# One over the RMS by columns, embedding products pinned between output projection and FFN, attention pools laid out anew: a float32 encoder kernel on one core

## The chip, the core and the metric

The kernel runs on one core of a Trainium2 chip. The metric is the device time of one launch in microseconds (us). Five engines work side by side, each on its own queue of instructions in a fixed order: PE (TensorE, matrix products), DVE (VectorE), ACT (ScalarE), POOL (GpSimd) and SP (SyncE), which here only issues DMA transfers. They wait for one another through semaphores, so an instruction that waits also holds all that stands behind it in its queue.

## What is computed

Two layers of an encoder over 1024 positions with 1024 channels, all in float32. Layer 0 has differential attention, layer 1 windowed attention with four query heads to one key head. Each layer runs:

```python
hn = rms_norm(h, attn_norm[i])
if i % N_MIXERS == 0:
    mix = diff_attention(hn, diff_w_qkv[j], diff_w_o[j], diff_lambda[j], diff_subln[j], cos, sin, i)
else:
    mix = windowed_gqa(hn, swa_w_qkv[j], swa_w_o[j], swa_sinks[j], cos, sin)
h = h + mix
h = h + conv_ffn(rms_norm(h, ffn_norm[i]), ffn_w_up[i], ffn_conv_w[i], ffn_conv_b[i], ffn_w_down[i])
gate = jax.nn.sigmoid(rms_norm(h, ple_norm[i]) @ ple_w_gate[i])
h = h + (p[i] @ ple_w_proj[i]) * gate
```

`rms_norm` divides each position by the root of its mean square. A last `rms_norm` follows layer 1. `p[i] @ ple_w_proj[i]` (1024 x 256 by 256 x 1024) is called the embedding product below; it needs nothing of `h`.

## The kernel before

Activations lie transposed: 8 tiles of 128 channels by 1024 positions, worked on in two halves (hf 0 and 1) of 512 positions. Every float32 operand is split into a high part (a cast on ACT) and a low part (a subtraction on DVE or POOL), and each product is three matmuls of 128 x 128 by 128 x 512 (`mm3`, L237 to L239). Weights come through a ring of buffers: raw `wr`, high `wh`, low `wl`, two of each. The up-projection computes its two-by-two blocks with seven products in place of eight (m1 to m7, L1107 to L1109), which need sums of the weights (`seven_weights`, L1071 to L1081, tiles sf, wd, w) and of the activations (`seven_begin`, `seven_rest`: tiles q, qb, ta, tb, qa, qu). Up-projection weights come in 22 groups, j.

The stages of a layer, in order: `qkv0` or `qkv1` (queries, keys, values, stored to memory), the attention (`diff_attn`, `swa`), `out_proj` with the residual add, the embedding product `p_proj`, `ffn_up`, `ffn_down`, and the gate (`ple0`, or `ple1_final` at the end). `projected` holds out_proj, p_proj and ffn_up together.

The order of the instructions on each engine is set by a scheduler ahead of time, from a program order and modelled durations; it is fixed then, and every queue runs in it. `out_proj` computes the first four row tiles for both halves, then the last four for half 0, then for half 1 (`half_order`). Each adds its old residual (read back from memory, `old`), squares the result on ACT (L472) and sums the squares on DVE into nacc (L473). When a half is complete, `norm_half` makes one over the RMS for it: a matmul of ones by nacc (L499) gives the sum over channels in every row of a 128 x 512 tile, DVE scales it (L500), ACT takes Ln (L502) and Exp (L503), each after a table load, and DVE makes a Newton step (L477 to L479). Where the same numbers are wanted as columns, four transposes (L511) and a copy (L512) turn them (`rstd_cols`). In `p_proj`, p is transposed on PE (L1282), split, and multiplied; the sums are copied by ACT (L1303) into two tiles pp of 128 x 1024 and stored. DVE then normalises the residual (L1010) for the up-projection.

Memory for the tiles of the attentions comes from pools with one place each (`attn_pools`); the order of the names decides which earlier tiles lie beneath a place, and so what its first load must wait for.

## Time and profile before

| | us |
|---|---|
| median of 3 runs | 2752.45 |
| lowest, highest | 2751.73, 2758.04 |
| the profiled execution, its own time | 2753.88 |
| its span, first to last instruction | 2752.1 |
| PE busy in it | 2633.3 |
| DVE, ACT, POOL busy | 1947.6, 1226.2, 1076.2 |
| mean granted clock of PE | 0.985 of 2.4 GHz |

Time between a row's start and the next start on the same engine tells what an instruction costs there; matmuls are pipelined, so the duration shown for one (about 0.39 us for 512 columns) is longer than the distance of two starts. A name such as `ps<-gh,wh` is the output tile and its inputs. What stands in brackets behind a row is the engine's idle time ahead of it and the instruction that ended the idle time.

### The profile page before, as it was taken

What the parts mean: (1) busy time and instruction counts of PE and PEld (TensorE: products, weight loads), DVE (VectorE), ACT (ScalarE), POOL (GpSimd) and SP (SyncE); (2) the same over time, 40 slices, a digit from 0 to 9 for tenths busy, and PEclk for the clock granted to TensorE, in tenths of its full rate; (3) what the DMA queues carried; (4) which work ended last, traced back from release to release, by engine and by line L of the source; (5) the groups of instructions that cost most, each with busy time, mean ns of one, the idle gap of its engine ahead of it and who ended that gap; (6) DMA issues with size and microseconds to landing.
All of it is one profiled execution on the core that took longest, in us unless ns stands there. A gap on an engine that the chain in (4) does not pass through costs nothing. (4 is left out here: it accounts for less than half of the span.)

```text
span 2752.1 us, 33264 instructions
## 1 busy us (share of the span) xinstructions
PE 2633.3 (96%) x12606; PEld 2184.3 (79%) x12606; DVE 1947.6 (71%) x2276; ACT 1226.2 (45%) x2133; POOL 1076.2 (39%) x609
## 2 busy tenths in 40 slices
PE   8999899999889999999999998999899999999998
PEld 6888788888678888878888787888678888788877
DVE  7640478784598888866677755874888888856664
ACT  5322577773444444441145525873444444421152
POOL 2642477774023443425312443441133434334201
PEclk9999999999999999999999999999899999999999
DMA  6445323303322323234314446103323223344112
GB/s 227 163 152 173 109 79 108 96 12 111 114 88 78 92 70 92 90 140 142 104 46 138 145 151 225 47 28 119 130 69 92 78 84 92 117 143 138 62 65 97
DMA packets 201828, 296.23 MB, mean 108 GB/s; under 512 B 9268, under 2 KB 138437, under 8 KB 197957
## 3 DMA queue, kind: packets, MB, share of 16 engines
q1 hardware_dynamic: 201045, 293.72, 32.5%
q8 instruction: 99, 1.62, 0.2%
q14 instruction: 60, 0.49, 0.1%
q10 hardware_dynamic: 624, 0.39, 0.0%
HBM read 207.83 MB, written 86.25 MB: 107 GB/s over the span
## 5 line engine op out<-in xcount | busy, mean ns | idle before, releaser
L148 POOL TENSOR_TENSOR wl<-wr,wh 128x1024 fp32r<-128x1024 f32 (+1 forms) x113 | 295.3, 2630 | 651.2 <-ACT wh L142 594.5
L1071 POOL TENSOR_TENSOR sf<-wr 128x1024 f32<-128x1024 f32 x42 | 136.2, 3244 | 549.9 <-DVE w L1081 549.9
L1237 DVE TENSOR_TENSOR res<-res,ps 128x512 f32<-128x512 f32 x320 | 217.0, 684 | 146.2 <-PE ps L239 143.5
L237 PE MATMUL ps<-gh,wh 128*128 128x512 f32 x704 | 272.9, 391 | 5.2 <-DVE ug L1178 4.0
L239 PE MATMUL ps<-gh,wl 128*128 128x512 f32 x704 | 274.4, 390 | 0.0
L238 PE MATMUL ps<-gl,wh 128*128 128x512 f32 x704 | 274.4, 390 | 0.0
L237 PE MATMUL ps<-hn,wh 128*128 128x512 f32 x544 | 215.1, 396 | 4.9 <-ACT wh L142 4.9
L238 PE MATMUL ps<-hn,wh 128*128 128x512 f32 x544 | 213.6, 393 | 0.0
L239 PE MATMUL ps<-hn,wl 128*128 128x512 f32 x544 | 212.9, 393 | 0.1
L142 ACT CAST wh<-wr 128x1024 fp32r<-128x1024 f32 (+1 forms) x140 | 144.7, 1091 | 124.2 <-PE ps L238 68.7
L748 ACT ACTIVATE e<-S,sm 128x1024 f32<-128x1024 f32 x128 | 142.4, 1114 | 92.8 <-DVE sm L744 91.0
L142 ACT CAST gh<-gr 128x1024 fp32r<-128x1024 f32 x44 | 46.1, 1051 | 295.4 <-PE ps L239 214.2
L1080 ACT CAST w<-sf 128x1024 fp32r<-128x1024 f32 x88 | 92.6, 1052 | 177.7 <-PE ps L1109 104.6
L744 DVE TENSOR_REDUCE sm<-S 128x1 f32<-128x1024 f32 x128 | 152.5, 1216 | 24.7 <-PE S L743 23.6
L237 PEld LDWEIGHTS ps<-gh,wh 128*128 128x128 f32 x704 | 132.2, 188 | 35.0 <-issue 4.8
L239 PEld LDWEIGHTS ps<-gh,wl 128*128 128x128 f32 x704 | 132.4, 188 | 27.5
L760 POOL TENSOR_TENSOR e<-e,e 128x1024 f32<-128x1024 f32 x64 | 152.1, 2377 | 5.3
L238 PEld LDWEIGHTS ps<-gl,wh 128*128 128x128 f32 x704 | 132.5, 188 | 27.1
L1107 PE MATMUL ps<-qb,w 128*128 128x512 f32 x352 | 138.7, 394 | 13.2 <-ACT pp L1303 9.9
L1109 PE MATMUL ps<-qa,w 128*128 128x512 f32 x352 | 138.0, 392 | 2.9 <-DVE w L1081 2.9
L1108 PE MATMUL ps<-qb,w 128*128 128x512 f32 x352 | 137.8, 392 | 0.0
L1108 PE MATMUL ps<-qa,w 128*128 128x512 f32 x352 | 137.7, 391 | 0.1
(260 smaller groups left out, 7283.0 us busy)
## 6 DMA issues: line engine op xcount, KB each, us to landing
wr<-ffn_w_up SPq DMA_DIRECT2D x88, 512.0 KB, 5.2
gs<-c SPq DMA_DIRECT2D x44, 512.0 KB, 2.9
wr<-ffn_w_down SPq DMA_DIRECT2D x22, 1024.0 KB, 5.1
gr<-gs SPq DMA_DIRECT2D x44, 512.0 KB, 3.7
qs<-rhl SPq DMA_DIRECT2D x32, 512.0 KB, 3.1
wr<-diff_w_qkv SPq DMA_DIRECT2D x12, 1024.0 KB, 5.9
ks<-rhl SPq DMA_DIRECT2D x20, 512.0 KB, 3.1
spill<-res SPq DMA_DIRECT2D x16, 512.0 KB, 2.6
```

What stands on the lines that cost most here:

```text
L142: self.nc.scalar.copy(out, in_)
L148: eng.tensor_tensor(out, in_, f32(hi), op=ALU.subtract)
L237: self.nc.tensor.matmul(out, ah, bh, start=first, stop=False)
L238: self.nc.tensor.matmul(out, ah, bl, start=False, stop=False)
L239: self.nc.tensor.matmul(out, al, bh, start=False, stop=last)
L744: v.tensor_reduce(sm[:, a : a + 1], ps[:], axis=AX.X, op=ALU.max, negate=True)
L748: nc.scalar.activation(e[:], ps[:], AF.Exp, bias=sm[:, a : a + 1], accum_out=sm[:, 2 + a : 3 + a])
L760: nc.gpsimd.tensor_tensor(ea[:], ea[:], eb[:], op=ALU.add)
L1107: mm(ps, ah, bh, start=first and i == 0, stop=False, skip_group_check=True)
L1108: mm(ps, ah, bl, start=False, stop=False, skip_group_check=True)
L1109: mm(ps, al, bh, start=False, stop=last and i == n - 1, skip_group_check=True)
L1237: v.tensor_tensor(self.res[dt][:, sl], self.res[dt][:, sl], acc[:], op=ALU.add)
```

## The change

1. **One over the RMS by columns.** `norm_half` becomes `norm_steps` and `spread_cols`. Four matmuls with one output column each (a 128 x 128 block of nacc as weights, a column of ones as data) give the sums as columns, 128 x 4. DVE scales them and POOL raises them to the power -1/2. DVE multiplies them into a diagonal matrix, a matmul of ones by it spreads them over all rows, and DVE copies the result. Ln, Exp, the Newton step and the transposes of `rstd_cols` are gone; `x_rstd` at the start uses the same spreading.
2. **The embedding product.** The transposes and splits of p go between the two halves of out_proj, its weights are fetched during half 1, and the 16 units of six matmuls run after out_proj, in memory pools of their own (three tiles pp of 128 x 512, 16 stores). The first matmul of each unit is kept in program order, and so are the norm's instructions of half 1: two units, the column matmuls, the remaining steps of `seven_begin`, two units, the spreading matmul, then twelve units. The first group of up-projection weights is fetched before the units, and its sums are on POOL (before, group 0 had them on DVE). In ffn_up's group 0, m1 and m2 are computed whole first. `old` has four buffers of its own.
3. **Attention pools.** New orders of places for both.
4. **Smaller pieces.** `ffn_down` takes its banks in another order and raises the priority of the loads of its first group; `qkv1`'s first weights are fetched and cast in `ple0`, between two blocks of half 1.

On PE, out_proj's end in layer 0 (ps is a sum's bank, wh and wl weights or parts of p, nacc the sum of squares). Before:

```order
L239 MATMUL ps_6288<-wh_6249,wl_6282 128x512
L239 MATMUL ps_6306<-wh_6249,wl_6282 128x512
L239 MATMUL ps_6314<-wh_6249,wl_6282 128x512
L499 MATMUL ps_6238<-nacc_5760,ones 128x512
L239 MATMUL ps_6324<-wh_6249,wl_6282 128x512
L239 MATMUL ps_6332<-wh_6249,wl_6282 128x512
L239 MATMUL ps_6342<-wh_6249,wl_6282 128x512
L239 MATMUL ps_6350<-wh_6249,wl_6282 128x512
L237 MATMUL ps_6360<-wh_6249,wh_6281 128x512
```

After (qb holds the parts of p now):

```order
L239 MATMUL ps_6366<-qb_5531,wh_6190 128x512
L242 MATMUL ps_6366<-qb_5531,wh_6190 128x512
L243 MATMUL ps_6366<-qb_5531,wl_6191 128x512
L239 MATMUL ps_6366<-qb_5532,wh_6190 128x512
L242 MATMUL ps_6366<-qb_5532,wh_6190 128x512
L243 MATMUL ps_6366<-qb_5532,wl_6191 128x512
L509 MATMUL ps_6375<-ones,nacc_5764 128x1 x4
L239 MATMUL ps_6390<-qb_5531,wh_6190 128x512
L242 MATMUL ps_6390<-qb_5531,wh_6190 128x512
```

The sum for the norm stood alone among products of p taken piece by piece; now its four column matmuls (the row with x4) stand between two whole units.

On SP, between qkv0 and the differential attention (vs is the store of v, stk a stack of queries or keys, wr a weight). Before:

```order
L646 DMA vs<-vf_1995 128x512
L646 DMA vs<-vf_2023 128x512
L646 DMA vs<-vf_2051 128x512
L646 DMA vs<-vf_2079 128x512
L620 DMA stk_2188<-qs_224 128x2048
L620 DMA stk_2189<-ks_228 128x2048
L169 DMA wr_5931<-diff_w_o 128x8x256
```

After:

```order
L642 DMA stk_2183<-ks_228 128x2048
L171 DMA wr_5797<-diff_w_o 128x8x256
L668 DMA vs<-vf_1905 128x512
L668 DMA vs<-vf_1933 128x512
L668 DMA vs<-vf_1961 128x512
L642 DMA stk_2182<-qs_224 128x2048
L644 DMA stk_2184<-ks_228 64x2048
L645 DMA stk_2184<-ks_228 64x2048
L743 DMA v_2189<-vs 128x8x128
L743 DMA v_2540<-vs 128x8x128
```

The loads of the stacks stood behind the stores of v; now they stand among them.

On DVE, the norm of half 1 in layer 0. Before:

```order
L148 TENSOR_TENSOR wl_6250<-ps_6251,wh_6249 128x512
L148 TENSOR_TENSOR wl_6250<-ps_6258,wh_6249 128x512
L473 TENSOR_TENSOR nacc_5760<-nacc_5760,old_6169 128x512
L148 TENSOR_TENSOR wl_6250<-ps_6265,wh_6249 128x512
L473 TENSOR_TENSOR nacc_5760<-nacc_5760,old_6200 128x512
L148 TENSOR_TENSOR wl_6250<-ps_6272,wh_6249 128x512
L473 TENSOR_TENSOR nacc_5760<-nacc_5760,old_6231 128x512
L500 TENSOR_SCALAR nv_6237<-ps_6238 128x512
L477 TENSOR_TENSOR nv_6237<-rstd_6241 128x512
L478 SCALAR_TENSOR_TENSOR nv_6237<-nv_6237 128x512
L479 SCALAR_TENSOR_TENSOR rstd_6241<-nv_6237,rstd_6241 128x512
```

After:

```order
L1121 TENSOR_TENSOR w_1069_6319<-wr_6312,w_1069_6319 128x1024
L480 TENSOR_TENSOR nacc_5764<-nacc_5764,old_6144 128x512
L993 TENSOR_TENSOR res_5730<-ps_6150,old_6175 128x512
L480 TENSOR_TENSOR nacc_5764<-nacc_5764,old_6175 128x512
L480 TENSOR_TENSOR nacc_5764<-nacc_5764,old_6221 128x512
L480 TENSOR_TENSOR nacc_5764<-nacc_5764,old_6259 128x512
L1121 TENSOR_TENSOR wd_6328<-wr_6312,wd_6328 128x512
L1121 TENSOR_TENSOR wd_6742<-wr_6726,wd_6742 128x512
L518 TENSOR_SCALAR rcol_6080<-ps_6375 128x4
L532 TENSOR_TENSOR diag_6409<-identr,rcol_6080 128x512
L542 COPY rstd_6413<-ps_6411 128x512
```

The splits of p (wl) between the sums are gone, and the splits of up-projection weights (w, wd) stand there; the rows from L500 to L479 gave way to three.

The diff, cut to its core:

```diff
+P_BANKS = ["b0", "b1", "b4", "b5", "b6", "b7"]
+DOWN_BANKS = ["b0", "b1", "b2", "b4", "b6", "b7", "b3", "b5"]
...
+    def kept(self, ins):
+
+        return self.tc.keep_in_program_order(ins)
...
+    def norm_steps(self, st, hf, psum, order, pin):
...
+        for i in range(4):
+            pin(
+                nc.tensor.matmul(
+                    ps[:, i : i + 1], acc[:, i * P : (i + 1) * P], self.ones[:, 0:1],
+                    start=True, stop=True,
+                )
+            )
...
+            nc.vector.tensor_scalar(
+                rc, ps[:, :4], 1.0 / D, EPS, op0=ALU.mult, op1=ALU.add
+            )
...
+        nc.gpsimd.tensor_tensor(rc, rc, self.mhalf[:, 0:1].to_broadcast([P, 4]), op=ALU.pow)
+        yield
...
+    def spread_cols(self, rc, hf, tp, psum, order, pin):
...
+            nc.vector.tensor_tensor(
+                dg[:].rearrange("p (i q) -> p i q", i=4),
+                self.ident.unsqueeze(1).to_broadcast([P, 4, P]),
+                rc.unsqueeze(2).to_broadcast([P, 4, P]),
+                op=ALU.mult,
+            )
...
+        pin(nc.tensor.matmul(ps[:], self.ones[:], dg[:], start=True, stop=True))
         y = self.rstd_tile(hf)
-        nc.scalar.activation(a, v, AF.Ln)
-        nc.scalar.activation(y[:], a, AF.Exp, scale=-0.5)
-        self.rsqrt_newton(y[:], v, a)
...
+        pin(nc.vector.tensor_copy(y[:], ps[:]))
...
-        for i in range(4):
-            self.nc.tensor.transpose(ps[:, i, :], rstd[:, i * P : (i + 1) * P], self.ident)
-        self.nc.vector.tensor_copy(rc[:, hf * 4 : hf * 4 + 4], ps[:, :, 0])
...
-            t = tp.tile([P, 2, HS], F32, tag="t", name=self.nm("old"))
+            old = tp.tile([P, HS], F32, tag="o", name=self.nm("old"))
...
+        def finish(psum, order, others):
+            steps = self.norm_steps(st, 1, psum, order, self.kept)
+            self.step(others)
+            self.step(others)
+            next(steps)
+            while begin:
+                self.step(begin)
+            self.step(others)
+            self.step(others)
+            for _ in steps:
+                pass
+            return st["rstd"]
...
-        eng = nc.vector if hurry else nc.gpsimd
+        eng = nc.gpsimd
...
-            w = self.seven_weights(raw, fp, j < 1)
+            w = first if j == 0 else self.up_weights(layer, j, fp)
...
+                for m in order[:2]:
+                    prod(pm[m], m)
                 for k in kps:
-                    for m in order:
+                    for m in order[2:]:
...
-                acc = self.bank(psum)
+                acc = self.bank(psum, DOWN_BANKS)
...
+                if g == 0:
+                    with self.tc.high_priority(400):
+                        load(j)
...
-                self.mm3(ps[:], terms)
-                nc.scalar.copy(t[:, sl], ps[:])
-                if hf == 1:
-                    nc.sync.dma_start(out[rs, :], t[:])
+                self.mm3(ps[:], terms, True)
+                nc.scalar.copy(t[:], ps[:])
+                nc.sync.dma_start(out[r * P : (r + 1) * P, sl], t[:])
...
+        def late():
+            self.hurry = True
+            self.wk1 = self.wrope(self.wraw(self.io["swa_w_qkv"][0], D))
+            self.hurry = False
...
+                first = self.up_weights(layer, 0, fp)
...
+                    rstd = finish(psum, END_BANKS, pieces)
+                    while pieces:
+                        self.step(pieces)
...
-            ap = self.attn_pools(c, "a0", ["q0", "k0", "l0", "q1", "k1", "l1"])
+            ap = self.attn_pools(c, "a0", ["k0", "q0", "l0", "v", "a", "k1", "q1", "l1", "e"])
...
-            ap = self.attn_pools(c, "a1", ["k0", "q0", "k1", "q1"])
+            ap = self.attn_pools(c, "a1", ["e", "a", "k1", "q1", "v", "k0", "q0"])
```

Before, `attn_pools` put `"v", "a", "e"` ahead of the names that it is given.

## Rows read from the trace of the kernel before

**Rows 1.** page, part 1: busy time, share of the span, instructions of each engine.

```profile
PE 2633.3 (96%) x12606; PEld 2184.3 (79%) x12606; DVE 1947.6 (71%) x2276; ACT 1226.2 (45%) x2133; POOL 1076.2 (39%) x609
```

**Rows 2.** waits of PE: line, what it waited for: us in all, times, longest.

```profile
PE S L742 <- DMA stk<-ks: 7.4, 1, 7.4
PE S L881 <- issue: 6.4, 1, 6.4
...
PE S L881 <- ACT e L894: 8.5, 5, 5.3
...
PE ps L237 <- ACT wh L142: 5.2, 3, 4.2
...
PE ps L511 <- DVE rstd L479: 4.3, 1, 4.3
PE ps L237 <- DVE ug L1178: 4.0, 2, 2.1
...
PE ps L237 <- DVE res L977: 12.2, 4, 5.5
PE ps L1107 <- ACT pp L1303: 9.9, 2, 5.0
```

**Rows 3.** stretches: length; busy us (instructions) by engine, PE first; PEclk, DMA share, GB/s.

```profile
1521.00:1532.00 11.00, 6.81 (x21) 4.95 (x20) 10.73 (x13) 9.44 (x9) 3.55 (x2) 0.72 0.38 141
1655.00:1700.00 45.00, 31.53 (x194) 28.99 (x194) 21.88 (x35) 21.43 (x61) 11.65 (x19) 0.85 0.66 245
1920.00:1980.00 60.00, 46.06 (x176) 35.18 (x175) 48.22 (x60) 31.86 (x49) 12.48 (x5) 0.86 0.41 136
2000.00:2020.00 20.00, 20.00 (x89) 16.45 (x88) 18.67 (x20) 9.87 (x10) 4.82 (x3) 1.00 0.26 79
2644.00:2656.00 12.00, 7.16 (x28) 4.77 (x27) 7.28 (x12) 4.92 (x8) 0.44 (x1) 0.86 0.00 0
```

**Rows 4.** timeline of DVE, layer 1, before FFN: start, us, instruction [idle, releaser].

```profile
1921.95 0.68 DVE L977 TENSOR_TENSOR res<-ps,old 128x512 f32<-128x512 f32 x1
...
1926.76 2.78 DVE L148 TENSOR_TENSOR q<-res,q 128x512 fp32r<-128x512 f32 x1
...
1936.41 0.67 DVE L473 TENSOR_TENSOR nacc<-nacc,old 128x512 f32<-128x512 f32 x1
...
1944.79 0.69 DVE L500 TENSOR_SCALAR nv<-ps 128x512 f32<-128x512 f32 x1 [7.71 <-PE ps L499]
...
1951.63 5.39 DVE L1010 SCALAR_TENSOR_TENSOR res<-res,par,rstd 128x512 f32<-128x512 f32 x8
```

**Rows 5.** timeline of ACT, same stretch.

```profile
1947.49 1.28 ACT L503 ACT_TABLE_LOAD   x1
1948.78 0.63 ACT L503 ACTIVATE rstd<-nv 128x512 f32<-128x512 f32 x1
```

**Rows 6.** timeline of PE, same stretch.

```profile
1925.74 0.49 PE L1282 MATMUL ps<-identr,wr 128*128 128x128 f32 x3
```

**Rows 7.** timeline of POOL, same stretch.

```profile
1926.63 5.11 POOL L148 TENSOR_TENSOR wl<-wr,wh 128x1024 fp32r<-128x1024 f32 x2 [40.39 <-ACT wh L142]
```

**Rows 8.** groups by line on POOL: busy, mean ns; idle before.

```profile
L1071 POOL TENSOR_TENSOR sf<-wr 128x1024 f32<-128x1024 f32 x42 | 136.2, 3244 | 549.9 <-DVE w L1081 549.9
...
L687 POOL TENSOR_TENSOR ss<-ss,mhalf 128x4 f32<-128x4 f32 x16 | 16.3, 1019 | 3.1 <-DVE ss L684 1.8
```

**Rows 9.** one line on PE: duration ns min/median/max, starts.

```profile
L499 PE MATMUL ps<-nacc,ones x20: 590/592/595, 703.9 to 2664.9; 128*128 128x512 f32 x20
```

**Rows 10.** timeline of SP, before both attentions.

```profile
295.33 0.32 SPq L620 DMA_DIRECT2D stk<-ks  x1
...
1655.51 0.80 SPq L620 DMA_DIRECT2D q<-qs  x2
```

**Rows 11.** timeline of ACT, first exponential of the windowed attention.

```profile
1676.88 0.48 ACT L894 ACTIVATE e<-S,sm 128x257 f32<-128x257 f32 x1 [10.01 <-DMA vs<-vhl]
```

**Rows 12.** page, part 6: DMA issues, KB each, median us to landing.

```profile
wr<-ffn_w_up SPq DMA_DIRECT2D x88, 512.0 KB, 5.2
```

More of the change, by code (lines that the diff above doesn't have):

```diff
@@ L236, in mm3 @@
             last = i == n - 1
-            self.nc.tensor.matmul(out, ah, bh, start=first, stop=False)
+            ins = self.nc.tensor.matmul(out, ah, bh, start=first, stop=False)
+            if keep and first:
+                self.kept(ins)
             self.nc.tensor.matmul(out, ah, bl, start=False, stop=False)
@@ L466, in norm_tile @@
         if st["acc"][hf] is None:
-            acc = st["tp"].tile([P, HS], F32, tag="n", name=self.nm("nacc"))
+            pool = st["keep"] if hf == 1 and st["keep"] else st["tp"]
+            acc = pool.tile([P, HS], F32, tag="n", name=self.nm("nacc"))
             st["acc"][hf] = acc
@@ L493, in norm_half @@
     def norm_half(self, st, hf, psum, order):
+        for _ in self.norm_steps(st, hf, psum, order, lambda ins: ins):
+            pass
+    def norm_steps(self, st, hf, psum, order, pin):
         nc = self.nc
-        t = st["tp"].tile([P, 2, HS], F32, tag="t", name=self.nm("nv"))
-        v, a = t[:, 0], t[:, 1]
         ps = self.bank(psum, order)
-        nc.tensor.matmul(ps[:], self.ones[:], st["acc"][hf][:], start=True, stop=True)
-        nc.vector.tensor_scalar(v, ps[:], 1.0 / D, EPS, op0=ALU.mult, op1=ALU.add)
@@ L501, in norm_half @@
[L501 to L512 removed]
+        acc = st["acc"][hf]
@@ L944, in swa, with out_proj @@
             self.step(jobs)
-    def out_proj(self, w, hp, tp, psum, which, layer):
+    def out_proj(self, w, hp, tp, keep, psum, which, layer):
         nc = self.nc
@@ L1003, in half_order @@
                     unit(b, c, hf)
+                if hf == 1 and b == 2 and late is not None:
+                    late()
             done(hf)
+            if hf == 0 and middle is not None:
+                middle()
     def normed(self, layer, kt, hf, rstd):
@@ L1263, in ffn_down, with p_parts @@
                     self.norm_half(st, hf, psum, END_BANKS)
[L1264 to L1269 removed]
+        return st["hn"], st["rstd"], st["cols"]
+    def p_parts(self, layer, psum):
         nc = self.nc
```

217 lines of the change are left out of this document (111 added, 106 removed).

## The prediction

> **What bounds the kernel now.** I read the busy shares first: PE is busy 96% of the span and the next engine, DVE, 71% [rows 1]. So only two things can shorten the program: fewer PE columns, or less time in which PE stands or runs slowly. The change hardly touches the columns, so the next view is what PE waited for [rows 2]. The waits that matter are few, long and each at a border between two stages: the differential attention's first tile (7.4 us), the two waits before the windowed attention (6.4 and 5.3), the first products of qkv1 (4.2), the last norm (4.3), the two ffn_up to ffn_down borders (4.0 together), and above all, in both layers, the border from out_proj over the embedding products to ffn_up (12.2 and 9.9 in all). The third view, stretches, shows that a wait costs more than its length, since the granted clock falls behind it: in the undisturbed stretch it is 1.00 and 89 matmuls take 20.00 us, 0.225 us each, at full clock (2.4 GHz); in the stretches with a wait the mean is 0.72 to 0.86, that is, part of each ran at the lower level, 1.2 GHz [rows 3].
>
> From these I take as lost, in a stretch, its length less 0.225 us for each of its matmuls. 1920 to 1980: 60 - 176 x 0.225 = 20.4, and about 22 since 16 of the 176 are 128-wide transposes of half that time; the list of waits has its two long waits twice, once in each layer, so layer 0 counts the same. 1521 to 1532: 11 - 21 x 0.225 = 6.3. 2644 to 2656: 5.7. The windowed attention's matmuls are of several widths, so there I go by idle time: 1655 to 1700 has 45 - 31.5 = 13.5 us without PE work, and clock 0.85 [rows 3].
>
> **The change part by part.** The sum is made against the profiled execution's own 2753.88 us (span 2752.1); the median of the runs is 2752.45, so 1.4 is taken off at the end.
>
> *(a) Attention pools, layer 0.* The first loads stk are issued one after the other, the second at 295.33, behind the last use of the memory under them, and PE waits 7.4 us [rows 2, 10]. In the new order the two loads stand in the middle of the v products, ahead of the last stores of v, so they land under PE work. What is late next is ACT, which casts output weights until about then. Gain 7.5, from 5 to 9 (with less slow clock behind it).
>
> *(d) Attention pools, layer 1.* Two loads q are issued together at 1655.51, and PE waits 6.4 us [rows 2, 10]; then the first exponential is held to 1676.88 by the store of v, because its tile e lies over v's source, and PE waits 5.3 more [rows 2, 11]. After the change only k0 and q0 are in front, q1 comes later, and e lies elsewhere. Together 11.7 us of waiting and perhaps 3 of slow clock. I don't credit all: k0 and q0 still follow the last projections over SP, and the first exponential now needs a table load, since no Exp ran in the norm before. That load is 1.28 us [rows 5]. Gain 8.5, from 3 to 10.
>
> In that row the load ends at 1948.77 and the activation starts at 1948.78 [rows 5], so nothing follows it. The Trainium skill, "ScalarE: Activation LUTs", section "What ACT_TABLE_LOAD costs", adds a drain of 1380 ns to the 1283 ns of the load, 2.66 us for each switch. By that the first exponential would be 1.4 us later and the result 2707 instead of 2706; the trace does not show the drain, so the row decides.
>
> *(c) ple0 to qkv1.* PE waits 4.2 us for the cast of the first qkv1 weights, because ACT first runs the table loads and activations of the norms and of the gate [rows 2]. Afterwards there are no Ln and Exp, and the weights are fetched and cast between two blocks of ple0's second half, 24 matmuls ahead (5.4 us). The stretch loses 6.3 [rows 3]. Gain 7 with the half-clock part that lies outside the window, from 3 to 7.5.
>
> *(f) ffn_down to ple1_final.* PE waits 4.3 us for rstd, whose columns it must transpose; the chain is sum, Ln, Exp, Newton [rows 2]. By columns the transposes are gone. What is late next is the cast of the gate weights, which I put at 1.5 us (three waits on such casts come to 5.2 [rows 2]). The stretch loses about 6 and the clock stays low a little longer. Gain 5, from 2 to 6.5.
>
> *(b) ffn_up to ffn_down.* Two waits of about 2 us on a bank whose reader, DVE's ug, is late [rows 2]. The new order of banks takes others first, and the loads of the first group are raised. What is late next is DVE's uv just ahead, a wait that stays. Gain 3 for both layers, from 0 to 4.
>
> *(e) out_proj, embedding products, ffn_up.* This is the largest term. Before, p is transposed, split on DVE and multiplied while the norm of half 1 runs on DVE and ACT. PE waits 5.5 for DVE [rows 2], whose queue is full until the last nacc sum at 1936.41 [rows 4]; then ones x acc, scale at 1944.79, Ln, Exp, Newton, and the normalisation starts only at 1951.63 [rows 4, 5]. The eight stores of p's products and their two tiles give the second wait, 5.0 [rows 2].
> Afterwards, on layer 1's clock: before, the transposes of p end near 1926.5 [rows 6]; they now come earlier and shift out_proj by as much, so it ends near there, 1926.9. Two units of six matmuls take 2.7, to 1929.6. The next instruction on PE is the four pinned one-column matmuls, and nothing may pass them. They need nacc. From 1921.95 [rows 4] DVE has 19 operations of 0.67 or, started one behind the other, 0.60 us, and one of double width: 12.7 us, to 1934.6. To this I add 2.1: an operation of 0.67 took 2.78 beside GpSimd's wl [rows 4, 7], and the first sum of the up-weights, 3.24 us on GpSimd [rows 8], now falls into this queue. So nacc is ready at 1936.7 and PE waits 7.1. Slow clock behind it 2.4 (as behind the 5.5 now), the small matmuls 0.9. Then scale, pow (1.02, the same shape [rows 8]), diagonal, one ones x diag matmul (two records of 0.59 [rows 9], as before) and a copy: rstd at about 1943 instead of 1951.6, with two units of p beside it. Then twelve units (16.3 us) run beside the normalisation (5.4 [rows 4], perhaps 2 more beside GpSimd's second and third sum), then m1 and m2 (5.4). The weights of the other products come when p's weights have freed their buffer: 5.2 us of loading [rows 12], a cast and a split, about 1.8 later than PE. Lost afterwards 7.1 + 2.4 + 0.9 + 1.8 = 12.2, and 12.5 with rounding up for ones x diag out of line. Gain 22 - 12.5 = 9.5 in each layer, 19 together; bounds 0 (the new waits are as long as the old) and 18 a layer (nacc is ready when PE gets there).
>
> *Costs.* Eight further norm halves get four one-column matmuls of two records each. No row shows such a record; it is between nothing and the 0.59 of the 512-wide one [rows 9]. I take 0.1, nearer to nothing because the width is 1 against 512: 0.8 a half, 6.4 in all, part of it inside waits, against 16 transposes removed (1.8). Cost 3, from -1 to 8 (0.59 each would be 38, which I hold for excluded, since the record would not shrink with its width at all). GpSimd's pow, ten times 1.02, lies beside PE work except in (e). The old loads issued earlier, and the 16 instead of 8 stores of p's products, lie on SP beside PE work: nothing, and some us in the prologue if that cover is gone.
>
> **Sum.** 7.5 + 8.5 + 7 + 5 + 3 + 19 - 3 = 47. 2753.9 - 47 = 2706.9; against the median 2705.5, so 2706.
>
> **Rivals.**
> R1, as summed: 2706.
> R2, the FFN border returns nothing. For it: PE's order is pinned, so each us by which DVE's queue or a weight is late is a us of PE, and PE waits there longer (7.1 against 5.5) by my own account. Against: rstd comes 8 us earlier. 2706 + 19 = 2725.
> R3, the border closes. For it: DVE may clear its queue earlier, as p's four splits (four of 0.6) are gone from it. 2 x 18 = 36 instead of 19: 2689.
> R4, the change doesn't do what it says at the attentions: the loads are early in the queue but wait for other memory under the new places, or for v. Then (a) and (d) are lost: 2706 + 16 = 2722.
> R5, slower: the first up-projection weights. Their load stands on SP behind out_proj's stores, its cast on ACT ahead of two squares, its split on DVE ahead of all nacc sums but one, and these ahead of PE's pinned matmuls. If the load is late, ACT, DVE, and PE stand in turn. Counted is landing near 1927.5, 5.2 us after its buffer is free [rows 12]. Each us later is one us of PE in each layer; the 47 are used up when it lands 24 us later, and it is slower by over 0.3% (8.3 us, about what a measurement of this kernel can tell) from 28 us. Only a buffer that is freed by the products of p themselves would do that. About 2765.
>
> **How the numbers follow.** Chances: R1 0.52, R2 0.22, R3 0.12, R4 0.08, R5 0.06. Predicted is R1, 2706. The low end is R3 with the better bounds of (a), (c) and (d), 2689 - 5 = 2684. The high end is R2 with the lower bounds of (b), (d), (f), about half of them coming at once: 2725 + 10 = 2735. Beyond lie R5 and parts of R2 to R4. Within 0.3% would need R2 and R4 together, and half of (c) and (f) gone, 0.05; faster by over 0.3% 0.89, slower 0.06.
>
> **What would show it.** In the profile after: no wait of PE for stk above 2 us, and none of 5 for e (a, d); no wait for the cast in qkv1 (c); no transposes of rstd (f); in each layer one wait of about 7 at the one-column matmuls, for nacc, and one under 2.5 at ffn_up's third product (e). It is wrong if the pinned matmuls wait over 12 us, if DVE's operations beside GpSimd's sums take 2.8 in a row, if the differential attention's steps, which I hold unchanged, take longer, or if the first exponential of the windowed attention starts no sooner behind the last v product.

## The result, and the profile after

| | before | after |
|---|---|---|
| median of five runs each, us | 2751.73 | 2730.89 |
| ratio, with its 95% interval | | 0.9924 (0.9907 to 0.9940) |
| span of the profiled execution, us | 2752.1 | 2728.9 |
| mean granted clock of PE | 0.985 | 0.989 |

The kernel became faster by 21 us (23 by the spans). 46 were forecast, so the sign and the range held and the size did not: less than half of it came. One disturbed run of the kernel after, 3293.94 us, is left out of the ratio.

Read as before the change, the page's first part of the kernel after comes first (busy time, share, instructions):

```profile
PE 2637.1 (97%) x12670; PEld 2189.5 (80%) x12670; DVE 1929.6 (71%) x2250; ACT 1185.6 (43%) x2090; POOL 1102.4 (40%) x625
```

ACT lost 41 us of work, DVE 18, and PE has 64 more matmul records than in [rows 1]. The bound is the same, so again it is the waits of PE that count. These are the ones that answer to [rows 2] (line, what it waited for: us in all, times, longest):

```profile
PE ps L509 <- DVE nacc L480: 9.5, 3, 4.3
PE ps L239 <- DVE qb L150: 7.0, 2, 3.6
PE ps L1147 <- ACT pp L1357: 5.8, 2, 3.6
...
PE ps L239 <- DVE rcol L518: 3.0, 1, 3.0
PE S L897 <- ACT e L910: 2.8, 5, 0.7
...
PE ps L242 <- DVE gl L150: 2.2, 3, 1.0
...
PE ps L239 <- ACT wh L144: 1.2, 2, 0.7
```

Gone are the 7.4 for stk, the 6.4 and the 5.3 ahead of the windowed attention, the 4.2 for qkv1's cast, the 4.3 for rstd at the end and the 4.0 for ug. New are two waits for qb, one in each layer, three at the column matmuls for nacc, one for rcol, three for gl. The rows of [rows 2] come to 58 us, these to 31.5; the span fell by 23.

The stretches that answer to [rows 3], of the kernel after (length; busy us and instructions of PE, PEld, DVE, ACT, POOL; PEclk, DMA share, GB/s):

```profile
1500.00:1520.00 20.00, 17.00 (x71) 13.38 (x70) 11.18 (x16) 8.42 (x10) 4.33 (x2) 0.91 0.31 110
1640.00:1685.00 45.00, 39.91 (x272) 36.33 (x271) 24.45 (x41) 25.93 (x69) 14.62 (x23) 0.96 0.87 298
...
1913.00:1926.00 13.00, 5.67 (x17) 3.74 (x15) 12.24 (x20) 6.29 (x11) 0.36 (x1) 0.84 0.65 202
1926.00:1935.00 9.00, 8.70 (x29) 6.96 (x30) 5.62 (x6) 2.56 (x4) 6.23 (x4) 0.66 0.08 31
1980.00:2000.00 20.00, 20.00 (x90) 16.57 (x89) 18.44 (x16) 10.27 (x11) 5.88 (x4) 1.00 0.26 79
```

The start of the windowed attention is repaired: 39.9 us of PE work in 45 against 31.5. The FFN border is not: behind out_proj PE works 5.7 us of 13, and then runs nine more at a mean clock of 0.66, most of them at 1.2 GHz.

Where the time went is best seen from one event on PE to the next, since PE does the same work between them. In us, worked out from the starts of PE's instructions; the columns behind "after - before" are kernels of the experiments below.

| stretch, up to | before | after - before | pools_alone - before | bank_skip - before | skip_nopin - before |
|---|---|---|---|---|---|
| first score of layer 0's attention | 302.7 | -6.7 | -7.7 | -7.7 | -7.5 |
| its last score | 320.8 | -2.7 | -2.8 | -2.9 | -3.4 |
| out_proj's last product | 96.3 | +5.1 | +4.4 | +5.0 | +5.2 |
| first product of ffn_up that reads qa | 50.9 | -5.0 | -1.3 | -10.3 | -14.0 |
| first product of ffn_down | 421.3 | -1.8 | +0.6 | -1.8 | +2.1 |
| first product of ple0 | 239.0 | +0.5 | +0.9 | +0.6 | -1.4 |
| last product of qkv1 | 232.1 | +4.0 | +0.6 | +5.6 | +5.7 |
| last score of layer 1's attention | 166.4 | -10.2 | -11.4 | -9.2 | -10.9 |
| out_proj's last product | 94.6 | +6.4 | +7.7 | +6.3 | +6.5 |
| first product of ffn_up that reads qa | 52.0 | -4.9 | -2.4 | -8.7 | -15.1 |
| first product of ffn_down | 421.4 | -6.0 | -0.4 | -6.0 | +2.0 |
| its last product | 257.1 | -1.9 | +0.7 | -1.9 | -4.0 |
| last product of all | 88.2 | +0.6 | +0.0 | +0.6 | +0.6 |

**The border, row by row.** On PE in layer 1, first the four groups of transposes of p, then each row ahead of which PE stood, and the matmuls of the norm (start, us, instruction, count, and in brackets the idle time and its releaser):

```profile
1888.45 1.04 PE L1324 MATMUL ps<-identr,wr 128*128 128x128 f32 x8
1900.53 0.60 PE L1324 MATMUL ps<-identr,wr 128*128 128x128 f32 x4
1908.02 0.60 PE L1324 MATMUL ps<-identr,wr 128*128 128x128 f32 x4
...
1917.43 0.50 PE L239 MATMUL ps<-wh,qb 128*128 128x512 f32 x1 [3.36 <-DVE qb L150]
1926.30 1.83 PE L509 MATMUL ps<-ones,nacc 128*128 128x1 f32 x8 [4.26 <-DVE nacc L480]
1932.75 1.02 PE L540 MATMUL ps<-diag,ones 128*128 128x512 f32 x2
...
1956.49 0.80 PE L1147 MATMUL ps<-qb,w 128*128 128x512 f32 x1 [3.64 <-ACT pp L1357]
```

The transposes don't come together. The third group is 12 us and the fourth 19.6 behind the first: their turn in the rotation of PSUM banks (the eight places for PE's sums) falls on two of them, b2 and b3, that hold half 0's column sums and its spread result, and these are free only when DVE has read them. PE doesn't stand at these rows, which have no bracket: the order that was set ahead of time puts them behind those reads (L518 at 1896.02, L542 at 1902.95). DVE in the same stretch:

```profile
1903.68 8.89 DVE L1050 SCALAR_TENSOR_TENSOR res<-res,par,rstd 128x512 f32<-128x512 f32 x8
...
1916.11 1.87 DVE L150 TENSOR_TENSOR qb<-ps,qb 128x512 fp32r<-128x512 f32 x3
...
1926.07 3.45 DVE L1121 TENSOR_TENSOR wd<-wr,wd 128x512 fp32r<-128x512 f32 x2
1929.44 0.15 DVE L518 TENSOR_SCALAR rcol<-ps 128x4 f32<-128x4 f32 x1
1930.72 1.76 DVE L532 TENSOR_TENSOR diag<-identr,rcol 128x512 f32<-128x512 f32 x1 [1.13 <-POOL rcol L522]
1934.73 1.23 DVE L1121 TENSOR_TENSOR w<-sf,w 128x1024 fp32r<-128x1024 f32 x1 [2.25 <-ACT w L1120]
1935.88 0.68 DVE L542 COPY rstd<-ps 128x512 f32<-128x512 f32 x1
1936.60 5.39 DVE L1050 SCALAR_TENSOR_TENSOR res<-res,par,rstd 128x512 f32<-128x512 f32 x8
```

Three of p's splits stand behind half 0's normalisation, at 1916.11, so out_proj is done at 1913.68 and the first unit of p starts at 1917.43. The eight normalisations take 8.89 us; they took 5.39 in [rows 4], and half 1's take 5.39 here at 1936.60. GpSimd shows what lies beside half 0's and not beside half 1's:

```profile
1902.83 5.22 POOL L150 TENSOR_TENSOR wl<-wr,wh 128x1024 fp32r<-128x1024 f32 x2 [5.54 <-ACT wh L144]
...
1925.64 2.72 POOL L1111 TENSOR_TENSOR sf<-wr 128x1024 f32<-128x1024 f32 x1 [17.60 <-DVE nacc L480]
1929.67 1.02 POOL L522 TENSOR_TENSOR rcol<-rcol,mhalf 128x4 f32<-128x4 f32 x1 [1.30 <-DVE rcol L518]
1930.66 1.28 POOL L1114 TENSOR_TENSOR sf<-sf,wr 128x512 f32<-128x512 f32 x1
```

The same happens to wd (3.45 us for two) beside sf at 1925.64 and to diag (1.76 instead of 0.69) beside sf at 1930.66. And rstd's copy, whose matmul is over near 1933.8, waits until 1935.88 behind a split of w that waits 2.25 us for its cast on ACT.

### The profile page after: what moved, and what is told of

Its sections match the earlier page's. It is cut to its first block, busy times and chain, and to the rows that moved or that the text cites. A ratio compares the mean times of both kernels' runs of the same rounds, so it can differ in the third digit from the quotient of the medians.

```text
span 2728.9 us, 33386 instructions
## 1 busy us (share of the span) xinstructions
PE 2637.1 (97%) x12670; PEld 2189.5 (80%) x12670; DVE 1929.6 (71%) x2250; ACT 1185.6 (43%) x2090; POOL 1102.4 (40%) x625
## 4 chain that ended last, share of the span: by engine, by line
PE 78%; DVE 10%; ACT 5%; issue 3%; DMA 2%; POOL 1%; SPq 0%; ACTq 0%; POOLq 0%; DVEq 0%
PE ps L239 13%; PE ps L242 13%; PE ps L243 13%; PE ps L1148 10%; PE ps L1149 10%; PE ps L1147 10%; PE ps L802 2%; ACT e L770 2%; DVE sm L766 1%; DVE ss L706 1%; PE S L764 1%; PE T L793 1%; PE S L765 1%; PE T L928 1%; DVE res L1050 1%
## 5 line engine op out<-in xcount | busy, mean ns | idle before, releaser
L1111 POOL TENSOR_TENSOR sf<-wr 128x1024 f32<-128x1024 f32 x44 | 146.8, 3336 | 542.4 <-DVE w L1121 507.2
L239 PE MATMUL ps<-gh,wh 128*128 128x512 f32 x704 | 274.7, 391 | 1.0 <-DVE rstd L542 0.8
L239 PE MATMUL ps<-hn,wh 128*128 128x512 f32 x544 | 214.4, 396 | 4.8 <-DVE rcol L518 3.0
L239 PEld LDWEIGHTS ps<-gh,wh 128*128 128x128 f32 x704 | 132.6, 188 | 30.2 <-DVE rstd L542 1.9
L1121 DVE TENSOR_TENSOR w<-sf,w 128x1024 fp32r<-128x1024 f32 x88 | 107.7, 1224 | 45.9 <-ACT w L1120 45.9
L1148 PE MATMUL ps<-qa,w 128*128 128x512 f32 x352 | 137.2, 390 | 0.9 <-DVE qa L150 0.9
```

The lines of the kernel that those rows point to most:

```text
L239: ins = self.nc.tensor.matmul(out, ah, bh, start=first, stop=False)
L1148: mm(ps, ah, bl, start=False, stop=False, skip_group_check=True)
```

## The experiments

All ratios are against the kernel before on the same chip. "The border" is the time from out_proj's last product to the start of ffn_up's 84th, layer 0 and layer 1: 64.7 and 65.3 us before, 63.4 and 60.4 after. A group of weights has 84 products; where nothing is kept in order, some of the second group's stand among them. (The expectations give 66.1 and 63.1 for the kernel after, and the like for others: that count left out the twelve products with wd and so ended 2 to 3 us later.)

### Parts of the change alone

**pools_alone**: the kernel before, with the new orders of places.

```diff
-        ap = Bank(ctx, self.tc, name, ["v", "a", "e"] + stacks)
-        return ap
+        return Bank(ctx, self.tc, name, stacks)
...
-            ap = self.attn_pools(c, "a0", ["q0", "k0", "l0", "q1", "k1", "l1"])
+            ap = self.attn_pools(c, "a0", ["k0", "q0", "l0", "v", "a", "k1", "q1", "l1", "e"])
...
-            ap = self.attn_pools(c, "a1", ["k0", "q0", "k1", "q1"])
+            ap = self.attn_pools(c, "a1", ["e", "a", "k1", "q1", "v", "k0", "q0"])
```

> The kernel before with nothing changed but the order of the places in both attentions' memory pools (parts (a) and (d) alone). Theory N (the two attentions carry the whole gain, all other parts together net about zero): the stretches up to the end of each attention lost 9.7 and 10.9 us less in the trace after, so this kernel gains about 20 of the 21 us, 2731 to 2733. Rival (the parts share the gain as the forecast had it, 16 of 47): 2736 or more, and the rest of the change is worth 5 or more.

Measured: 2742.34 against 2755.53 us, ratio 0.9948 (0.9931 to 0.9964), span 2741.0: 11 by the spans and 13 by the medians. That is in the rival's range: the pools bring half to two thirds of the whole change, not nearly all of it. The table shows the rest of their gain being returned: 11.4 us are won in the stretch up to the last score of layer 1, and 7.7 given back in the out_proj behind it. Of these, 4.4 are idle time, most of it a wait for GpSimd's last scaling of e and one for an operand of out_proj; the granted clock, 1.00 there before, is 0.92 from 1813 to 1835 (timeline of PE, pools_alone):

```profile
1820.25 1.91 PE L912 MATMUL T<-identr,e 128*128 128x128 f32 x8 [2.68 <-POOL e L900]
1827.17 1.20 PE L237 MATMUL ps<-xo,wh 128*128 128x512 f32 x4 [1.25 <-ACT xo L142]
```

**norm_alone**: the kernel before, with the norm by columns and the spreading, all else as it was.

```diff
-        nc.tensor.matmul(ps[:], self.ones[:], st["acc"][hf][:], start=True, stop=True)
...
+        for i in range(4):
+            nc.tensor.matmul(
+                ps[:, i : i + 1], acc[:, i * P : (i + 1) * P], self.ones[:, 0:1],
+                start=True, stop=True,
+            )
...
+        nc.gpsimd.tensor_tensor(rc, rc, self.mhalf[:, 0:1].to_broadcast([P, 4]), op=ALU.pow)
...
+        nc.tensor.matmul(ps[:], self.ones[:], dg[:], start=True, stop=True)
...
-        nc.scalar.activation(a, v, AF.Ln)
-        nc.scalar.activation(y[:], a, AF.Exp, scale=-0.5)
-        self.rsqrt_newton(y[:], v, a)
+        nc.vector.tensor_copy(y[:], ps[:])
```

> The kernel before with one over the RMS by columns as its only change (no Ln, Exp, Newton step, no transposes of rstd). Theory D (DVE's queue and the casts bound the borders, the norm's chain hardly does): the table loads leave ACT's queue in front of qkv1's first cast and the last norm, 4 to 6 us, while the column matmuls cost 0.9 us in each of ten halves: 2748 to 2754 on a chip where the kernel before takes 2752. Rival (the forecast's terms: 7 for qkv1, 5 for the last norm, some of the FFN border, less 3): 2740 or less.

Measured: ratio 1.0010 (1.0000 to 1.0019) over ten runs. Theory D held: taken alone, ten pairs of Ln and Exp less, with their table loads, are worth nothing. What it wins at the last norm and at layer 1's border it pays for with the column matmuls, 80 records, and with waits that the scheduler's new order has elsewhere (PE, norm_alone):

```profile
PE S L893 <- ACT e L906: 10.1, 5, 6.9
...
PE S L893 <- DMA q<-qs: 7.9, 1, 7.9
...
PE ps L1119 <- ACT w L1092: 7.3, 2, 6.3
```

**no_late**: the kernel after, with qkv1's first weights fetched and cast where they were before.

```diff
-        self.half_order(self.io["ple_w_gate"][0], blocks, unit, done, None, late)
+        self.half_order(self.io["ple_w_gate"][0], blocks, unit, done)
...
+        self.hurry = True
+        wk = self.wrope(self.wraw(w, D))
+        self.hurry = False
         for hf in range(2):
```

> The changed kernel, but qkv1's first weights are fetched and cast after ple0's norms as before, not between two blocks of its second half. Theory M (the early cast, 4 us on ACT, stands ahead of the last sigmoids, and GpSimd's split beside it holds DVE's residual operations, which take 3.4 instead of 0.7 us; so the wait was only moved): no loss, 2727 to 2733. Rival (the early cast is worth what was forecast): 2735 to 2738.

Measured: ratio 0.9921 (0.9904 to 0.9937), as with it. The early cast is worth nothing: with Ln and Exp gone, PE's products wait for a weight's cast 0.7 us at most (L239, wh) here as in the kernel after.

### What holds PE at the FFN border

**p_early**: the transposes and splits of p are written ahead of half 0's norm.

```diff
-            done(hf)
             if hf == 0 and middle is not None:
                 middle()
+            done(hf)
```

> The changed kernel, but the transposes and splits of p stand ahead of the norm of half 0, not behind it, so DVE's three late splits of p leave the queue in front of PE's first product of p. Theory D (DVE's queue bounds the whole border from out_proj to ffn_up; a wait that goes comes back later): the wait of 3.5 us at the first product goes, but only three splits of 0.6 us leave the full stretch, so 2 us a layer, 4 in all: about 2727. Rival O (the wait itself is lost time): wait and slow clock go, 4.5 a layer, 9 in all: about 2722.

Measured: ratio 0.9886 (0.9871 to 0.9900), span 2720.1, 8.8 below the kernel after. The wait for qb is gone from PE's list, and the longest at the column matmuls grows from 4.3 to 6.9; the border is 60.5 and 58.4, 5.0 less in both layers together, near theory D's 4 and not rival O's 9, though the time alone looks like O's 2722. That part speaks for p's splits; the rest was won in places that have nothing to do with p, 1.9 of it in layer 1's ffn_down.

**bank_skip**: the order stays, but behind each norm that `norm_half` makes (all but half 1's between out_proj and ffn_up) PE's next product passes over the two banks that hold the norm.

```diff
         for _ in self.norm_steps(st, hf, psum, order, lambda ins: ins):
             pass
+        while BANKS[psum.turn % len(BANKS)] in order:
+            psum.turn += 1
```

> The changed kernel, but after each norm the next product of PE does not take one of the two PSUM banks in which the norm's column sums and spread result lie. Theory B (in ple0 PE waits 3.0 us only because its next bank holds the column sums that DVE reads late): the wait at the third unit of half 1 and the slow clock behind it go, 5 us: 2726. Rival G (DVE stands there because the embedding product's load is late, and would hold the next bank as well): 2730 to 2732.

Measured: ratio 0.9885 (0.9871 to 0.9900), span 2721.1. PE's timeline in layer 1 shows the cause taken away: all transposes are over within 5.4 us, and the wait for qb is gone; what is left is the wait at the column matmuls.

```profile
1884.47 1.47 PE L1326 MATMUL ps<-identr,wr 128*128 128x128 f32 x12
1889.21 0.60 PE L1326 MATMUL ps<-identr,wr 128*128 128x128 f32 x4
...
1918.14 1.87 PE L511 MATMUL ps<-ones,nacc 128*128 128x1 f32 x8 [5.42 <-DVE nacc L480]
```

The border is 58.0 and 56.6, 9.2 less in both layers together. The expectation was about ple0 alone, and there the wait for rcol did go, but a longer one, 5.1 at the column matmuls, came in its place: the time fell further than expected, but not where it was expected. So the collision of banks is shown for the border, by two edits that undo it in different ways; it cost 5 to 9 us there, both layers together.

**dve_relief**: the low parts of half 0's activations are not computed on DVE but filled by copies on ACT, so the result lacks them.

```diff
-                self.two_parts(o, src)
+                self.copy_hi(o[:, 0], src)
+                self.copy_hi(o[:, 1], src)
```

> The changed kernel, but the low parts of half 0's normalised residual, eight splits of 0.6 us on DVE in each layer, are copies on ACT instead, so these low parts are left out of the result. Theory D: DVE bounds the border, so PE reaches the last product of ffn_up's first group about 4.8 us earlier in each layer (from 66.1 and 63.1 us after out_proj's last matmul to 61 and 58): about 2720. Rival P (PE is held by its own order, not by DVE): under 2 us a layer, 2727 or more.

Measured, in one run: span 2724.7, 4.2 below the kernel after, between the two expectations. The waits for qb have shrunk from 7.0 to 1.6 us in all, and the longest for nacc has grown to 6.0. DVE's list of work is a part of the border's length, but eight operations less on it, with eight more on ACT, shorten the border by only 2.5 and 1.2 us.

**no_pin**: nothing is kept in program order.

```diff
-        return self.tc.keep_in_program_order(ins)
+        return ins
```

> The changed kernel without keeping any instruction in program order, so that the scheduler may put products of p where the column matmuls wait. Theory D (DVE bounds the border): no gain, 2728 to 2735, the wait of 4.5 us at the column matmuls turns up at the first products of ffn_up. Rival P (the pinned order holds PE): the waits of 4.3 in both layers and their slow clock go, 9 to 12 us: 2719 to 2722.

Measured: ratio 0.9903 (0.9888 to 0.9918); not told apart from the kernel after. The border is 57.7 and 56.8, 5.7 and 3.6 us shorter, and about all of it is given back by the first product of ffn_down: PE stands for qa and, at ffn_down, for ug again.

```profile
PE ps L1147 <- ACT qa L144: 12.0, 2, 7.3
...
PE ps L239 <- DVE ug L1221: 6.3, 2, 3.2
```

So the kept order is not what costs the forecast its size.

**skip_nopin**: bank_skip and no_pin together.

```diff
+        while BANKS[psum.turn % len(BANKS)] in order:
+            psum.turn += 1
...
-        return self.tc.keep_in_program_order(ins)
+        return ins
```

> The changed kernel with both edits: no bank collision after a norm, and nothing kept in program order. Theory D: the border is full on DVE, so the two gains don't add; as the kernel with the banks alone, 2721 to 2726. Rival (pins and banks are separate costs): 2716 or less.

Measured: ratio 0.9891 (0.9876 to 0.9906), span 2717.2. In the border the two gains nearly add (53.0 and 52.5), which the theory of one cost behind both did not allow. In the time they don't: the ratio is that of bank_skip, and the table has +2.1 and +2.0 ahead of ffn_down, where PE waits 3.0 and 3.3 for ug.

**skip_normpin**: bank_skip, with the units of p free and only the norm's instructions kept.

```diff
-                self.mm3(ps[:], terms, True)
+                self.mm3(ps[:], terms)
```

> The bank skip of bank_skip, with the first product of each unit of p free to be moved, and only the norm's instructions of half 1 still kept in program order. In bank_skip, 5.58 us are lost at the column matmuls in each layer (716.8 and 1912.3); in skip_nopin, where nothing is kept, that wait is gone, 7.1 and 6.0 us are lost at m2's first product for qa instead, and 3.2 and 3.4 at ffn_down's first product for ug. Theory U: it is the pin on the units that holds the column matmuls too early. Then this run has no wait at the column matmuls of the layers' borders, since 6 to 7 units stand ahead of them, and since the norm's chain on DVE and the spreading matmul still stand in the order of the program, the wait for qa is shorter than in skip_nopin, 2 to 5 us; the stretch from out_proj's last product to the end of group 0 of ffn_up is 51 to 55 us (bank_skip 60.8 and 59.3, skip_nopin 55.0 and 54.5), and the span 2710 to 2717. Rival V: the qa wait belongs to DVE's list of work, which is as long either way (four low parts of the embedding's weights, normalisations, splits of weight sums); then 6 to 7 us are lost at qa as in skip_nopin, the stretch is 54 to 56 us, and the span 2716 to 2719. In both, ffn_down's wait for ug tells whether it hangs on the pins: 0 to 1 if on the norm's pins, 3.2 to 3.4 if on those of the units.

Measured: ratio 0.9888 (0.9871 to 0.9904), span 2722.4, border 53.2 and 52.4, waits for qa 13.0 in all and for ug 6.3. That is rival V in the border, with the numbers of skip_nopin; the spans of all four runs, 2720.4 to 2722.4, lie above both ranges. It is the kept first matmuls of the units that hold the column matmuls early and that spare ffn_down its wait, and without them PE reaches ffn_up sooner than DVE can. Skip_nopin's rows of ACT, then DVE, show that limit in layer 0:

```profile
749.76 1.05 ACT L144 CAST qa<-ta 128x1024 fp32r<-128x1024 f32 x1 [6.48 <-DVE tb L1094]
```

```profile
734.18 5.39 DVE L1052 SCALAR_TENSOR_TENSOR res<-res,par,rstd 128x512 f32<-128x512 f32 x8
...
748.99 1.28 DVE L1094 TENSOR_TENSOR tb<-ta,res 128x512 f32<-128x512 f32 x2
```

From rstd to the sums that qa is cast from, DVE works through without a pause for 16 us.

### GpSimd beside DVE

**sn_sfdve**: skip_nopin, with the sums of ffn_up's first group of weights on DVE as before the change.

```diff
-        eng = nc.gpsimd
+        eng = nc.vector if hurry else nc.gpsimd
```

> The kernel with neither bank collision nor pins (span 2717.2), but the sums of ffn_up's first weights on DVE as before the change, not on GpSimd. Theory G (beside GpSimd, DVE's operations take up to four times as long, so moving the sums gave DVE little): within 2 us of 2717. Rival (the move relieved DVE by 2.4 us a layer): 2721 or more.

Measured, in one run: span 2718.0 against 2717.2. No difference that one run could tell.

**sn_wldve**: skip_nopin, with all low parts of the embedding's weights on DVE, none on GpSimd.

```diff
-        if self.hurry and i % 2 == 1:
+        if self.hurry == 2 or self.hurry and i % 2 == 1:
...
+        self.hurry = 2
...
+        self.hurry = False
```

> The kernel with neither bank collision nor pins (span 2717.2), but the low parts of the embedding weights are all made by DVE, so that GpSimd doesn't run beside the normalisation of half 0. Theory G: the eight normalisations take 5.4 us again instead of 8.9, two splits of 1.2 come in, so 1 us a layer is gained: 2714 to 2717. Rival (GpSimd costs DVE nothing, and DVE gets 2.4 us more work a layer): 2720 or more.

Measured, in one run: span 2730.1, 12.9 worse. Theory G's mechanism held, its sum did not: with GpSimd idle from 1901.3 to 1922.0, the eight normalisations of half 0 take 5.38 again (DVE, layer 1).

```profile
1906.90 1.28 DVE L150 TENSOR_TENSOR wl<-wr,wh 128x512 fp32r<-128x512 f32 x2
...
1908.70 1.28 DVE L150 TENSOR_TENSOR wl<-wr,wh 128x512 fp32r<-128x512 f32 x2
...
1910.51 5.38 DVE L1052 SCALAR_TENSOR_TENSOR res<-res,par,rstd 128x512 f32<-128x512 f32 x8
```

But they stand behind four splits that were GpSimd's, and PE waits 15.3 and 8.1 us for qa. Most of the loss is in layer 0 (border 60.2 against 53.0; in layer 1, 53.3 against 52.5), where DVE also stands 5.0 us for the spreading matmul. So the program with the 3.5 us lost beside GpSimd is the faster one; how much of the 12.9 the splits themselves cost is not shown.

### The border from ple0 to qkv1

**sn_sig**: skip_nopin, with the gate's sigmoids in the last rows kept ahead of the casts of qkv1's weights on ACT.

```diff
+            cp = self.nc.scalar.copy(hv[:, t], rv[:, t])
+            if self.pinw:
+                self.tc.keep_in_program_order(cp)
...
-            nc.scalar.activation(t[:, 0], t[:, 0], AF.Sigmoid)
+            sg = nc.scalar.activation(t[:, 0], t[:, 0], AF.Sigmoid)
+            if hf == 1 and b >= 2:
+                self.tc.keep_in_program_order(sg)
```

> The kernel with neither bank collision nor pins (profiled span 2717.2), and in ple0's last units the sigmoids are kept ahead of the casts of qkv1's first two weight blocks on ACT. Theory S (the casts, 4 us each, stand ahead of the last residual's chain and make the wait of 5.1 at the column matmuls of half 1): the wait falls by 3 to 5, span 2712 to 2714. Rival W (the weights are then late by as much): 2716 to 2719.

Measured: ratio 0.9891 (0.9874 to 0.9907), that of skip_nopin, no gain. The wait at the column matmuls fell from 5.1 to 0.6, and this came instead (timeline of PE, sn_sig):

```profile
1519.56 1.02 PE L514 MATMUL ps<-ones,nacc 128*128 128x1 f32 x8 [0.58 <-DVE nacc L483]
1539.04 0.80 PE L242 MATMUL ps<-hn,wh 128*128 128x512 f32 x1 [5.86 <-ACT wh L212]
```

Whichever of the two ACT does first, PE waits five to six us for the other.

## Why the prediction was off by half

Two steps failed. (c) forecast 7 us from ple0 to qkv1, and none came. (e) forecast 19 at the FFN borders, and 6.3 came. (a), (d) and (f) were right in what they took away and too large in what they credited.

**What bounds the kernel** held: PE is busy 97% of the span, and the time moved with its waits and its clock.

**(a) and (d), the pools: right in their places, not in the sum.** At layer 0's first score 6.7 us were won (7.5 forecast), up to layer 1's last score 10.2 (8.5). The wait for stk is gone, the first exponential no longer waits 10 us for a store; it does have the table load in front, and it follows that load at once, as in [rows 5] (timeline of ACT, after):

```profile
1660.37 1.28 ACT L910 ACT_TABLE_LOAD   x1
1661.66 0.48 ACT L910 ACTIVATE e<-S,sm 128x257 f32<-128x257 f32 x1
```

What the step left out is the other end of the attention. Out_proj took 2.8 and 4.1 us longer than before for the same work (the table's +5.1 and +6.4, less 2.3 of transposes and column matmuls that moved into it); 1.4 and 2.5 of that are idle time. Alone, the pools bring 11 to 13, not 16. I looked for what is late next at the start of the attention only.

**(c), ple0 to qkv1: the step that failed outright.** From 7 forecast, none came: the stretches from ffn_down to qkv1's end are 4.5 us longer after, 1.5 with the pools alone, and some 2 of the 3.0 between are the work of the column and spreading matmuls, less the transposes that went. The wait for the cast is gone as forecast, and 3.0 for rcol came: the bank with the column sums is wanted again by the next product while DVE has its scaling queued behind a row of the gate. With that cured (bank_skip) it is 5.1 for nacc, and with that cured (sn_sig) 5.9 for the cast. As I read the order, behind all three stands one chain, the last residual to the sum to the rstd to qkv1's first product, with the gate's sigmoids and the weights' casts in one queue on ACT; no run took the whole chain away. I named ACT's Ln and Exp as the cause since they ended the wait; they were one of several things on it. No_late shows the same from the other side: the edit that was to bring these 7 can be undone for nothing.

**(e) and (b), the FFN borders: 14.9 instead of 22** (in each layer the three stretches from the last score to ffn_down's first product, against those of pools_alone). The sum hides where it came from. Up to ffn_up's 252nd product, the end of the work of three groups, 1.0 us was won in layer 0 and 5.3 in layer 1: that is (e), 6.3 instead of 19. The fourth group brought 4.3, 2.1 or 2.2 in each layer, that no term had: a wait of PE for a split of weights that was there before in both layers, at 826.29 and 2030.40, and is gone. That is luck. In PE's list before it is in this row:

```profile
PE ps L1109 <- DVE w L1081: 2.9, 3, 1.3
```

The remaining 4.3 are (b), for which 3 were forecast. Step by step on layer 1, from out_proj's end:

- Two units at once, then 7.1 of waiting at the column matmuls. Measured: 3.4 for qb, two units at the lower clock in 4.6 instead of 2.7, then 4.3. That is 9.6 lost ahead of the column matmuls, 7.7 of it waiting, and not 7.1, and nacc was ready 12.5 us after out_proj's end, not 9.8. The prediction took p's parts as ready and did not ask which banks its transposes would get.
- From nacc to half 1's normalisation: 6.3 forecast, 10.4 measured (14.6 before). The eight column records ran at the lower clock (1.83 us; granted 0.50 from 1926 to 1928), the scaling stood 1.3 us behind the split of wd, the diagonal took 1.76 beside GpSimd's sum, and the copy waited 2.1 behind the split of w. I had put 2.1 us of contention ahead of nacc and none behind it. These 4.1 us are the largest part of the miss in layer 1.
- Afterwards 1.8 for a weight. Measured 3.6 in layer 1, for a copy to pp that stands on ACT behind casts of qa, qu and w.
- Layer 0 missed more, 1.0 instead of 9.5. Its waits for qb and nacc are as long (3.6 and 4.3), and that for pp is 2.1; but two for qa follow that layer 1 does not have, and the granted clock is 0.89 from 760.9 to 778.8, where it is 1.00 in the like stretch of layer 1 (1960.5 to 1974.1). The cast of qa at 771.61 stands on ACT behind one of w, and that waited 9.92 us for GpSimd's sum of the second group; in layer 1 qa's last cast, at 1963.81, stands ahead of that of w. This is read from the trace alone, no run was made for it. PE, then ACT, layer 0:

```profile
772.71 0.50 PE L1147 MATMUL ps<-qa,w 128*128 128x512 f32 x1 [0.92 <-ACT qa L144]
774.15 0.50 PE L1148 MATMUL ps<-qa,w 128*128 128x512 f32 x1 [0.95 <-DVE qa L150]
```

```profile
770.66 1.05 ACT L1120 CAST w<-sf 128x1024 fp32r<-128x1024 f32 x1 [9.92 <-POOL sf L1115]
```

- At ffn_down, (b) came about as forecast: the 4.0 for ug are gone, and 2.2 for gl, in three waits of at most 1.0, are new.

The remark that the prediction would be wrong "if DVE's operations beside GpSimd's sums take 2.8 in a row" is what came about in a mild form: eight of them beside wl took 1.1 each instead of 0.67. On the mechanism, the Trainium skill, "GPSIMD Engine Reference", section "Key points", says that GpSimd shares its interfaces to SBUF, the memory that holds the tiles, with VectorE, and that it contends with VectorE's instructions that have two inputs there. The trace agrees, with 8.89 us beside GpSimd and 5.38 without.

**(f), the last norm: 2.1 instead of 5**, by the last two stretches against those of pools_alone. The wait for rstd is gone; 0.9 us of PE work came for it, and the chain of sum, GpSimd's power, diagonal and spreading is still on the path.

**Costs: the price was right.** Eight one-column records in ple0, the product behind them, and the weight loads that go with them:

```profile
1503.26 0.94 PE L509 MATMUL ps<-ones,nacc 128*128 128x1 f32 x8
1504.07 0.48 PE L243 MATMUL ps<-hn,wl 128*128 128x512 f32 x1
```

```profile
1503.04 1.08 PEld L509 LDWEIGHTS ps<-ones,nacc 128*128 128x128 f32 x8
```

From the first at 1503.26 to the next product PE takes 0.81 us, 0.10 a record, as I took it; ten halves make 8.1, less 1.8 for the transposes. What I took off because some of them would lie inside waits can't be separated here; at 0.81 the eight halves outside of (e) cost 6.5 less 1.8, which is 4.7 instead of 3. The weight loads are no faster than that: eight in 1.08 us. The Trainium skill, "TensorE: Matmul & The Clock Gate", section "LDWEIGHTS (loading the stationary operand)", makes a weight load a matter of its columns, columns / 1.2 in ns; for 128 columns that gives 107 ns, an estimate that the measured 0.10 a record agrees with.

**The rivals.** R2 put the FFN border's return at nothing, R1 at all of its 19; with 6.3 it was in between, nearer to R2, and the time, 2730.89, lies beyond R2's 2725. R4 was wrong as it stood: the loads do come early. No rival had the two other things that happened, a gain that is returned at the far end of the attention, and a wait that changes its name in qkv1. Misses in us: pools 5, (c) with the costs 7 (4 forecast, 3 lost), (e) and (b) 7 (13 missed in (e), 1 more than forecast in (b), 4 by luck), (f) 3, and 2 in the attentions' stretches, where the kernel after wins less than the pools alone: 24, the difference between the forecast 47 and the 23 of the spans.

**A better version.** The two lines of bank_skip make the ratio 0.9885 (0.9871 to 0.9900), against 0.9924 (0.9907 to 0.9940) for the kernel after; p_early does the same by order. Taking the pins away as well shortens the border by 5.0 and 4.1 us more and changes no time that these runs can tell.

What stays open: how much of (f)'s miss is DVE's queue and how much GpSimd's power, for which no run was made; and whether the border's last 5 us, with DVE busy throughout, can be had by giving DVE less to do, since dve_relief was only tried with the pins.

## What to carry to other kernels

When a short result is put into a PSUM bank between two groups of products, look up whose turn that bank is next: here two banks held for DVE delayed products that had nothing to do with the norm, and undoing that shortened the border by 5 to 9 us in two layers. Where a wait ends on one instruction, list what else in the same chain would end it within a few us, and credit the gain only down to the next of these; a stage that starts sooner also has to be followed to its end. Count DVE work with two inputs at its price beside GpSimd wherever the change puts the two side by side, not only where the trace of before shows it.

## What the runs showed of the hardware

- A one-column float32 matmul costs about as much as its weight load: 0.10 us a record at full clock (eight weight loads take 1.08), 0.21 at the lower one (from 1926.30 to the next product at 1927.99, 1.69 us for eight).
- Beside GpSimd's sums and low parts, DVE operations of 0.67 to 0.69 us took 1.1 on average over eight, a single one 1.76, and two splits of wd 3.45 (two operations of this size take 1.28 without).
- All but seven of the table loads are gone and ACT has 41 us less to do, without any effect on the time by that alone (norm_alone, 1.0010): ACT was waited for at a few places only, and where the wait for it went, another came.
